# Fewer units by the seven-product scheme in the second stage, and the table sums moved to POOL, in a fused neighbourhood-attention layer

## The chip, the core and the metric

The kernel runs on one core of a Trainium2 chip. The core has a matrix engine (TensorE, PE in the profile, with its weight loads as PEld), three engines for elementwise work (VectorE or DVE, ScalarE or ACT, GpSimd or POOL), and a queue processor (SyncE, SP) from which this kernel issues nearly all of its transfers. TensorE writes only into PSUM, eight banks of 128 x 512 float32 values here, which VectorE or ScalarE must empty before a bank can be used again. Each engine works through its own instructions in program order, and engines wait for each other on semaphores. The metric is the device time of one execution in microseconds (us); less is better.

## The reference

What must be computed is one layer (DEPTH is 1, so the second mixer is not reached): an RMS norm, one projection into query, key, value and gate, an attention over an 8 x 16 neighbourhood on a grid of 32 rows by 64 columns with a learned bias per head, a gate, an output projection, the residual and a last RMS norm, all in float32.

```python
S, D, H, HD = 2048, 1024, 16, 64          # tokens, width, heads, head size

def rmsnorm(x, g):
    y = x * rsqrt(mean(x * x, -1) + 1e-6)
    return y * g

h = rmsnorm(x, norm_0)
q, k, v, gate = split(h @ w_in_0, 4)       # w_in_0: (1024, 4096)
# for every query of the grid: keys of 8 rows by 16 columns around it (clipped at the border)
s = q . k / sqrt(64) + rpb_0[head, row offset, column offset]
o = softmax(s) @ v
x = x + (o * silu(gate)) @ w_out_0
out = rmsnorm(x, norm_f)
```

## The kernel before

**Precision.** Every float32 operand of a matmul is split into a rounded high part and the rest (`h` and `l`: ScalarE copies to the high part, then a subtraction gives the low part), and a product is three matmuls: h.h, h.l and l.h.

**Units and stages.** The projection is cut into *units* `(kind, j)`: kind is k, q, g or v, and j (0 to 3) picks four heads, that is two of the eight head pairs p. The tokens are four chunks of 512, two for each stage.

- *Stage one* (`stage_one`, up to about 416 us with the values of stage two) computes the values of all heads and all twelve units k, q, g for chunks 0 and 1.
- *Stage two* (`stage_two`) does the same for chunks 2 and 3, but only for the units in `units_two` (L224): j = 0 and 1, so six units.
- The other six units of chunks 2 and 3 (`halves`, L225) are left as *filler* for the attention.

The units of both stages go through `seven_products` (L388): for two blocks of weights by two chunks it forms seven sums or differences of blocks, so that seven products of 12 matmuls (84) take the place of eight (96). The sums of weights (L410), the splits (L403, L404), and the additions on the results (L428, L432, L438, L439) are elementwise work for it. The filler does its units in the plain way, 96 matmuls for a unit (`group`, L356; lines L365, L367, L369), from weights that `use_item` splits when they are due (L177, L178).

**The attention** is a loop of 64 *pieces* (and two iterations to drain it): `order` (L878) lists row tiles (p, T) of a head pair p and a quarter T of the grid, and each has two pieces of two column blocks. T = 0 comes first for all p, then T = 1 and 2, then T = 3. In iteration i:

- `begin(i)` queues loads: on an even i the keys of the next row tile, in each the value tiles of piece i (L923).
- `feed` issues filler matmuls, 45% of the piece's amount, `middle(i)` follows, then the other 55%. `amount` (L1248) is 768 / 48 = 16 matmuls in the first 48 pieces and 354 / 18 = 19.7 in the last ones. When the units are used up (after 576 matmuls), `feed` goes on with the output projection (`outputs`, L1226 to L1230).
- `middle(i)`, on even i, splits the queries (`split_q`; `ql` at L499) and, where the head pair or the type of row tile is new, makes its *table* with `bias` (L940): six sums `em` (L948) of a bias tile `e` and a mask, for three column types and two heads, three on POOL and three on VectorE. It also queues the load of the next head pair's `e` (L936).
- then `normalise(i - 1)` (VectorE's reciprocal L982, POOL's L984), `turns(i - 2)` (transposes on TensorE, L989, copied from PSUM by ScalarE, L1013, and VectorE, L1014, into `pta`), `scores(i)` (TensorE L966 into four banks `s`; VectorE L973 adds the table `em`; ScalarE's exp L976), and `values(i - 2)` (TensorE L1034).

**Evictions and late work.** A filler product that is done is emptied by VectorE (`tmp`, L326 or L328), and one of the output by L1138 (`y`). Work that should come later is put in a list with a due mark that counts matmuls (`store`): for an output row block the root of the norm on VectorE (L1154 to L1161) is due at 12, the scale by it (L1168 on VectorE, L1169 on ScalarE, L1170 on POOL) at 16, the store at 44. POOL also makes the low part of some weights (L178), of w_out (L183) and, in the attention, of keys (L352).

**Buffers.** Each pool has a fixed number of buffers: `vp` 6 (value tiles, and landing places in the stages), `ep` 2 (tables' `e`, and one result of the seven products).

Of the kernel before, what the change touches and what calls it, by code (L numbers as in the profile page):

```python
# [10 lines left out]
F32 = mybir.dt.float32  # L11
# [59 lines left out]
def build(ctx, tc, x, xr, xt, wg, rpb, w_out, n0, nf, masks, out):  # L71
# [19 lines left out]
    qp = pool("qp", 4)  # L91
    vp = pool("vp", 6)
    sp = pool("sp", 2)
# [3 lines left out]
    mp = pool("mp", 6)  # L97
    ep = pool("ep", 2)
    lp = pool("lp", 1)
# [58 lines left out]
    def use_item(it):  # L158
        kind, a, b = it
        state["event"] = clock[0]  # L160
        t = raws.pop(it)
        if kind == "x":
            split_x(a, b, t, (hh[a, b], hl[a, b]))
        elif kind == "w":
            u, ph = a
            if KINDS["v"] <= u < KINDS["g"]:
                t = t.rearrange("p (k c) -> p k c", c=256)
                a = u // 2 * 2, ph
                if u % 2 == 0:
# [7 lines left out]
            nc.scalar.activation(h, t, AF.Copy)  # L177
            (nc.gpsimd if (b + u) % 2 and attending[0] else nc.vector).tensor_tensor(l, t, h.bitcast(F32), OP.subtract)  # L178
        else:
            h, l = xs([128, 512], F32R, "woh"), xs([128, 512], F32R, "wol")  # L180
            woh[a, b], wol[a, b] = h, l
            nc.scalar.activation(h, t, AF.Copy)
            (nc.gpsimd if b else nc.vector).tensor_tensor(l, t, h.bitcast(F32), OP.subtract)  # L183

# [38 lines left out]

    units_two = [(k, j) for j in range(2) for k in "kqg"]  # L224
    halves = [(k, j, 1, c) for j in range(2, 4) for g in (("k", "q", "g") if j == 2 else ("k", "qg")) for c in (2, 3) for k in g]  # L225
    attending = [False]
# [107 lines left out]
    def give(kind, hp, c, tmp):  # L334
# [16 lines left out]
        nc.scalar.activation(hi, tmp, AF.Copy)  # L351
        (nc.gpsimd if attending[0] else nc.vector).tensor_tensor(lo, tmp, hi.bitcast(F32), OP.subtract)  # L352
        store(("k", hp, c), 12, lambda: (nc.sync.dma_start(k_hi[hp][:, s], hi.bitcast(F32)),
# [188 lines left out]
    def stage_one():  # L542
# [6 lines left out]
        land["x21"] = [spot[:, k] for k in range(3)] + [lp([128, 512], F32, "land")]  # L549
        slots = [(mp, 512)] * 6 + [(vp, 512)] * 2 + [(sp, 512)] * 2 + [(pa, 768)] * 2 + [(vp, 512)] * 4  # L550
        slots += [(qp, 512)] * 4 + [(kp, 960)] * 4
# [22 lines left out]
        def also(n, i):  # L574
# [15 lines left out]
            if n == 0:  # L590
# [6 lines left out]
                elif i == 1:  # L597
                    L2["x21"] = [p([128, 512], F32, "land") for p in (mp, mp, vp, vp)]
                    for k in range(4):
# [72 lines left out]
        load_rows(*halves_of(1)[4:])  # L672
        for a, b in ((0, 2), (1, 2)):
            load_v0(1, a, b)
        for b in range(4):
# [8 lines left out]
            else:  # L684
                split_v(1, 0, b)
                split_v(1, 1, b)
            if b == 1:
                for a in range(2):
                    load_v0(1, a, 3)
        for k in range(4):  # L690
# [50 lines left out]
    def stage_two():  # L741
        x12, x11, x21 = L2["x12"], L2["x11"], L2["x21"]
        x22 = [qp([128, 512], F32, "land") for _ in range(4)]
        for k in range(4):
            load_x(2, "x22", k, x22[k])
        slots = {"T2": [(mp, 512)] * 4 + [(kp, 960)] * 4,
                 "T3": [(sp, 512)] * 2 + [(pa, 768)] * 2 + [(qp, 512)] * 3 + [(lp, 512)],
                 "T4": [(vp, 512)] * 4 + [(mp, 512)] * 2 + [(vp, 512), (qp, 512)]}

# [190 lines left out]
    def bias(p, ty, cty):  # L940
# [4 lines left out]
        for s in range(2):  # L945
            t = mp([128, 512], F32, "em")[:, :n]
            EM[p, ty, cty, s] = t
            (nc.vector if s else nc.gpsimd).tensor_tensor(  # L948
                sh(t), E[p, s][:, u0 + 4:u1 + 4, v0 + 8:v1 + 8], sh(MK[0][:, m0:m0 + n]), OP.add)
# [196 lines left out]
    def finish(n):  # L1146
# [30 lines left out]
        store(("y", n), 12, root)  # L1177
        store(("y", n), 16, scale)
        store(("y", n), 44, send)
# [99 lines left out]
    def begin(i):  # L1279
        all_loads()  # L1280
        m = i // 2
        if i % 2 == 0 and m + 1 < len(order):
            kh, _, kl = LOADS[m + 1] = load_qk(*order[m + 1])
            later_loads([kh, kl], 0, 2)
        if i < N:
            p, T, cs = pairs[i]
            later_loads(load_v(p, T, cs[0]) + load_v(p, T, cs[1]), 1, 1.5)
        if i % 2 == 0 and 2 <= i <= N:
            p, T = order[m - 1]
            later_loads([lambda: load_sg(p, T)], 7, 0)  # L1290

    def middle(i):
        if i % 2 or i >= N:
            return
        m = i // 2
        p, T = order[m]
        ty = ROW_TYPE[T]
        for key in [key for key in EM if key[:2] != (p, ty)]:
            del EM[key]
        if type(QT[p, T]) is not tuple:  # L1300
            split_q(p, T)
        for cty in range(3):
# [67 lines left out]
```

## Time and profile before

| what | us |
|---|---|
| median of 3 runs (1141.05 to 1146.37) | 1145.77 |
| the profiled execution, its own time | 1150.48 |
| its span, first to last instruction | 1148.7 |
| busy PE / PEld | 1100.1 / 894.9 |
| busy DVE / ACT / POOL | 768.5 / 537.4 / 358.0 |
| first scores of the attention begin at | 533.9 |
| last scores (first of the last group) begin at | 1075.6 |

Busy time is the union of an engine's instructions. A matmul is recorded for longer than the distance to the next one, since they are pipelined, so a busy TensorE isn't one at its peak. The profile also gives the granted clock of TensorE (1 is full speed) for each stretch. In a row of the timeline, the first numbers are start and length in us, and a bracket at the end tells how long the engine was idle before it and what ended that. In a row of groups, `x576 | 186.3, 389 | 0.0` is a count, the busy time in us, the mean of one in ns, and the idle time before.

### The profile page before, as it was taken

What the parts mean: (1) busy time and instruction counts of PE and PEld (TensorE: products, weight loads), DVE (VectorE), ACT (ScalarE), POOL (GpSimd) and SP (SyncE); (2) the same over time, 40 slices, a digit from 0 to 9 for tenths busy, and PEclk for the clock granted to TensorE, in tenths of its full rate; (3) what the DMA queues carried; (4) which work ended last, traced back from release to release, by engine and by line L of the source; (5) the groups of instructions that cost most, each with busy time, mean ns of one, the idle gap of its engine ahead of it and who ended that gap; (6) DMA issues with size and microseconds to landing.
All of it is one profiled execution on the core that took longest, in us unless ns stands there. A gap on an engine that the chain in (4) does not pass through costs nothing.

```text
span 1148.7 us, 22549 instructions
## 1 busy us (share of the span) xinstructions
PE 1100.1 (96%) x7621; PEld 894.9 (78%) x7621; DVE 768.5 (67%) x1743; ACT 537.4 (47%) x1348; POOL 358.0 (31%) x439
## 2 busy tenths in 40 slices
PE   9999999999999999999899999999888899999997
PEld 6788888888888888887777777778666778877885
DVE  5376787888785357877565666657867676776644
ACT  7544433343353433334544556546655456545422
POOL 0000222222210003133653535534464444444300
PEclk9999999999999999999898989999989899998999
DMA  8634545353572335349887778789897687887542
GB/s 305 190 92 125 186 127 184 120 176 114 176 238 79 100 86 162 99 138 290 238 238 221 221 232 227 230 240 263 227 267 227 175 241 241 245 250 223 155 147 73
DMA packets 142962, 217.28 MB, mean 189 GB/s; under 512 B 18048, under 2 KB 65408, under 8 KB 142848
## 3 DMA queue, kind: packets, MB, share of 16 engines
q1 hardware_dynamic: 142704, 215.58, 62.6%
q8 instruction: 61, 1.00, 0.4%
q14 instruction: 53, 0.43, 0.1%
q10 hardware_dynamic: 144, 0.26, 0.1%
HBM read 157.05 MB, written 58.72 MB: 188 GB/s over the span
## 4 chain that ended last, share of the span: by engine, by line
PE 79%; DMA 6%; DVE 6%; ACT 4%; issue 3%; SPq 1%; POOL 0%; DVEq 0%; ACTq 0%
PE pp L421 29%; PE pv L534 11%; PE o L1034 7%; PE s L966 6%; PE po L1230 5%; PE po L1228 4%; PE po L1226 4%; PE pp L369 3%; PE ph L989 3%; PE pp L365 3%; PE pp L367 3%; DVE em L948 2%; DMA vt<-vd 1%; DMA raw<-in_wg_dram 1%; ACT x L976 1%
## 5 line engine op out<-in xcount | busy, mean ns | idle before, releaser
L439 POOL TENSOR_TENSOR tmp<-tmp,rb 128x512 f32<-128x512 f32 x54 | 88.2, 1634 | 442.9 <-DVE tmp L438 288.0
L984 POOL TENSOR_SCALAR x<-x,st 128x360 f32<-128x360 f32 (+5 forms) x256 | 143.7, 580 | 169.8 <-DVE st L982 127.2
L421 PE MATMUL pp<-h,f 128*128 128x512 f32 x576 | 186.3, 389 | 0.0
L976 ACT ACTIVATE x<-x,st 128x360 f32<-128x360 f32 (+5 forms) x256 | 151.7, 594 | 58.4 <-DVE st L973 58.4
L421 PE MATMUL pp<-t,f 128*128 128x512 f32 x648 | 155.8, 389 | 0.1
L421 PEld LDWEIGHTS pp<-t,f 128*128 128x128 f32 x648 | 121.6, 188 | 25.7 <-DVE u L432 0.6
L973 DVE CUSTOM_DVE_ANT_0 x<-s,em 128x360 f32<-128x360 f32 (+5 forms) x256 | 123.9, 537 | 5.5 <-PE s L966 2.9
L421 PEld LDWEIGHTS pp<-h,f 128*128 128x128 f32 x576 | 108.1, 188 | 22.3
L966 PE MATMUL s<-kt,qh 64*128 64x480 f32 (+5 forms) x512 | 88.5, 380 | 29.9 <-DVE y L1138 11.6
L1034 PEld LDWEIGHTS o<-pta,vt 96*64 96x64 f32 (+2 forms) x1792 | 95.9, 152 | 21.4 <-issue 11.6
L421 PE MATMUL pp<-l,f 128*128 128x512 f32 x288 | 112.0, 389 | 0.0
L1034 PE MATMUL o<-pta,vt 96*64 96x128 f32 (+4 forms) x1792 | 105.0, 275 | 3.5 <-DMA raw<-in_w_out_dram 1.0
L1230 PE MATMUL po<-wol,gh 128*128 128x512 f32 x252 | 102.5, 407 | 0.0
L1228 PE MATMUL po<-woh,gl 128*128 128x512 f32 x252 | 101.0, 401 | 0.0
L1226 PE MATMUL po<-woh,gh 128*128 128x512 f32 x252 | 101.0, 401 | 0.0
L1013 ACT ACTIVATE pta<-ph 96x256 f32<-96x256 f32 (+1 forms) x224 | 58.3, 332 | 86.2 <-PE ph L989 86.0
L1014 DVE COPY pta<-ph 128x384 f32<-128x384 f32 (+3 forms) x128 | 60.3, 511 | 53.9 <-PE ph L989 53.9
L534 PE MATMUL pv<-wh,h 128*128 128x512 f32 x256 | 88.3, 390 | 0.9 <-ACT wh L516 0.9
L534 PE MATMUL pv<-wl,h 128*128 128x512 f32 x256 | 88.0, 390 | 0.3 <-DVE wl L517 0.3
L534 PE MATMUL pv<-wh,l 128*128 128x512 f32 x256 | 88.0, 389 | 0.0
L404 DVE TENSOR_TENSOR f<-raw,f 128x512 fp32r<-128x512 f32 x90 | 72.6, 806 | 22.7 <-ACT f L403 22.7
L966 PEld LDWEIGHTS s<-kt,qh 64*128 64x128 f32 x512 | 51.4, 192 | 40.3 <-ACT pta L1013 14.5
(139 smaller groups left out, 2017.2 us busy)
## 6 DMA issues: line engine op xcount, KB each, us to landing
raw<-in_wg_dram SPq DMA_DIRECT2D x126, 256.0 KB
e<-in_rpb_dram SPq DMA_DIRECT2D x54, 240.0 KB
vt<-vd SPq DMA_DIRECT2D x256, 48.0 KB
row<-in_xr_dram SPq DMA_DIRECT2D x32, 256.0 KB
vd<-v SPq DMA_DIRECT2D x32, 256.0 KB
k_hi<-hi SPq DMA_DIRECT2D x32, 256.0 KB
k_lo<-lo SPq DMA_DIRECT2D x32, 256.0 KB
qd<-tmp SPq DMA_DIRECT2D x32, 256.0 KB
```

The costliest lines, as they stand in the source:

```text
L404: nc.vector.tensor_tensor(t[:, 1], src, t[:, 0].bitcast(F32), OP.subtract)
L421: nc.tensor.matmul(B[n, P], t[:, int(m == 2), c], x[k][int(m == 1)], start=P in (1, 6, 5) and k == 0 and m == 0, stop=k == 3 and m == 2, s ...
L439: nc.gpsimd.tensor_tensor(lay(tmp), lay(tmp), of(rb[c]), OP.mult)
L534: nc.tensor.matmul(ps[t], a[:, o], b, start=k == 0 and m == 0, stop=k == NK - 1 and m == 2)
L966: nc.tensor.matmul(pst[s], qq[a, qs], kk[a, :r1 - r0, c0:c1], start=(m == 0), stop=(m == 2))
L973: nc.vector.tensor_tensor_reduce(X[i, C][s], pst[s], EM[p, ROW_TYPE[T], COL_TYPE[C], s], -1.0, 1e38, OP.add, OP.min, st[:, s:s + 1])
L976: nc.scalar.activation(X[i, C][s], X[i, C][s], AF.Exp, bias=st[:, s:s + 1], scale=-1.0, accum_out=st[:, 2 + s:3 + s])
L984: nc.gpsimd.tensor_scalar(X[i, C][s], X[i, C][s], st[:, 4 + s:5 + s], 0.5, op0=OP.mult, op1=OP.mult)
L1034: nc.tensor.matmul(o[s * 64:s * 64 + 64, C * 128 + q0:C * 128 + q0 + nq], vt[C][:k, g - g0_, s * 64:s * 64 + 64], t[:k, at:at + nq], start ...
L1226: nc.tensor.matmul(p, gh, woh[q, j], start=(i == 0), stop=False)
L1228: nc.tensor.matmul(p, gl, woh[q, j], start=False, stop=False)
L1230: nc.tensor.matmul(p, gh, wol[q, j], start=False, stop=(i == NK - 1))
```

## The change

- `units_two` keeps j = 0 only: three units by seven products in stage two, nine plain ones as filler. `amount`, worked out from it, becomes 1056 / 48 = 22 in the first 48 pieces; the later ones keep 19.7.
- In the attention all six sums of a table are on POOL, and `bias` is called at the beginning of an even piece, in `begin`, not after 45% of its filler in `middle`. The load of the next `e` moves to `begin` too, with four `ep` buffers.
- The low parts of weights, of w_out and of keys are on VectorE alone.
- Value tiles are loaded for piece i - 1 in `begin(i)`, no longer for piece i, with four `vp` buffers. Some landing places and operands in the two stages move from `vp` to `ep`.
- Two value weights of stage one are loaded earlier, into `ev` buffers.
- The scale of an output row block is due at 24, not 16.

```diff
-    vp = pool("vp", 6)
+    vp = pool("vp", 4)
...
-    ep = pool("ep", 2)
+    ep = pool("ep", 4)
...
-            (nc.gpsimd if (b + u) % 2 and attending[0] else nc.vector).tensor_tensor(l, t, h.bitcast(F32), OP.subtract)
+            nc.vector.tensor_tensor(l, t, h.bitcast(F32), OP.subtract)
...
-            (nc.gpsimd if b else nc.vector).tensor_tensor(l, t, h.bitcast(F32), OP.subtract)
+            nc.vector.tensor_tensor(l, t, h.bitcast(F32), OP.subtract)
...
-    units_two = [(k, j) for j in range(2) for k in "kqg"]
-    halves = [(k, j, 1, c) for j in range(2, 4) for g in (("k", "q", "g") if j == 2 else ("k", "qg")) for c in (2, 3) for k in g]
+    units_two = [(k, j) for j in range(1) for k in "kqg"]
+    halves = [(k, j, 1, c) for j in range(1, 4) for g in (("k", "q", "g") if j < 3 else ("k", "qg")) for c in (2, 3) for k in g]
...
-        (nc.gpsimd if attending[0] else nc.vector).tensor_tensor(lo, tmp, hi.bitcast(F32), OP.subtract)
+        nc.vector.tensor_tensor(lo, tmp, hi.bitcast(F32), OP.subtract)
...
-        for a, b in ((0, 2), (1, 2)):
-            load_v0(1, a, b)
+        for a, b in ((0, 2), (1, 2), (0, 3), (1, 3)):
+            load_v0(1, a, b, ev([128, 512], F32, "raw") if b == 3 else None)
...
-            (nc.vector if s else nc.gpsimd).tensor_tensor(
+            (nc.gpsimd if attending[0] or not s else nc.vector).tensor_tensor(
                 sh(t), E[p, s][:, u0 + 4:u1 + 4, v0 + 8:v1 + 8], sh(MK[0][:, m0:m0 + n]), OP.add)
...
-        store(("y", n), 16, scale)
+        store(("y", n), 24, scale)
...
     def begin(i):
         all_loads()
         m = i // 2
-        if i % 2 == 0 and m + 1 < len(order):
-            kh, _, kl = LOADS[m + 1] = load_qk(*order[m + 1])
-            later_loads([kh, kl], 0, 2)
-        if i < N:
-            p, T, cs = pairs[i]
+        if i % 2 == 0 and i < N:
+            p, T = order[m]
+            ty = ROW_TYPE[T]
+            for key in [key for key in EM if key[:2] != (p, ty)]:
+                del EM[key]
+            for cty in range(3):
+                if (p, ty, cty, 0) not in EM:
+                    bias(p, ty, cty)
+            if m + 1 < len(order):
+                nx = order[m + 1]
+                LOADS[m + 1] = kh, _, kl = load_qk(*nx)
+                later_loads([kh, kl], 0, 2)
+                if nx[0] != p:
+                    later_loads(load_e(nx[0]), 4, 2)
+        if 0 < i <= N:
+            p, T, cs = pairs[i - 1]
             later_loads(load_v(p, T, cs[0]) + load_v(p, T, cs[1]), 1, 1.5)
...
     def middle(i):
...
-        p, T = order[m]
-        ty = ROW_TYPE[T]
-        for key in [key for key in EM if key[:2] != (p, ty)]:
-            del EM[key]
-        if type(QT[p, T]) is not tuple:
-            split_q(p, T)
-        for cty in range(3):
-            if (p, ty, cty, 0) not in EM:
-                bias(p, ty, cty)
+        if type(QT[order[m]]) is not tuple:
+            split_q(*order[m])
         if m + 1 < len(order):
-            nx = order[m + 1]
-            fs = load_e(nx[0]) if nx[0] != p else []
-            later_loads(fs + [LOADS[m + 1][1]], 1, 2)
+            later_loads([LOADS[m + 1][1]], 1, 0)
```

What this does to the engines' rows is shown at three places. A row is the line, the operation, and what it writes and reads, with its shape; the changed kernel's lines from `stage_one`'s end on are smaller by three, so its `em` is L945, its scale L1166.

VectorE in piece 16, the first with T = 1, from the gating of the former row tile (`og`) to the copies of `pta`; first before:

```order
L1048 TENSOR_TENSOR og<-o,sgt 128x512
L499 SCALAR_TENSOR_TENSOR ql<-qr,qh 128x512
L948 TENSOR_TENSOR em<-e,mk 128x360
L948 TENSOR_TENSOR em<-e,mk 128x480
L948 TENSOR_TENSOR em<-e,mk 128x360
L328 TENSOR_TENSOR tmp<-pp,rb 128x512
L341 SCALAR_TENSOR_TENSOR sg<-sg,tmp 128x512
L178 TENSOR_TENSOR w<-raw,w 128x512
L982 RECIPROCAL st<-st 128x2 x2
```

and in the changed kernel:

```order
L1045 TENSOR_TENSOR og<-o,sgt 128x512
L178 TENSOR_TENSOR w<-raw,w 128x512
L326 TENSOR_TENSOR tmp<-pp,rb 128x512
L352 TENSOR_TENSOR lo<-tmp,hi 128x512
L178 TENSOR_TENSOR w<-raw,w 128x512
L499 SCALAR_TENSOR_TENSOR ql<-qr,qh 128x512
L979 RECIPROCAL st<-st 128x2 x2
```

The three table sums ahead of the eviction `tmp` are gone; a second weight sum and the low part of a key have come, around the eviction.

POOL around the same table; before, with the normalisations of piece 14 ahead and those of piece 15 behind:

```order
L984 TENSOR_SCALAR x_6495<-x_6495,st 128x352
L984 TENSOR_SCALAR x_6496<-x_6496,st 128x352
L178 TENSOR_TENSOR w<-raw,w 128x512
L948 TENSOR_TENSOR em<-e,mk 128x360
L948 TENSOR_TENSOR em<-e,mk 128x480
L948 TENSOR_TENSOR em<-e,mk 128x360
L984 TENSOR_SCALAR x_6602<-x_6602,st 128x352
```

and in the changed kernel:

```order
L981 TENSOR_SCALAR x_6165<-x_6165,st 128x352
L981 TENSOR_SCALAR x_6166<-x_6166,st 128x352
L945 TENSOR_TENSOR em<-e,mk 128x360 x2
L945 TENSOR_TENSOR em<-e,mk 128x480 x2
L945 TENSOR_TENSOR em<-e,mk 128x360 x2
L981 TENSOR_SCALAR x_6280<-x_6280,st 128x352
```

Six sums stand where three stood, and the weight sum ahead of them, which waits for ScalarE, is gone.

ScalarE where the first output row block is scaled (`y`), from the query split to the copies of `pta`; before:

```order
L498 ACTIVATE qh<-qr 128x512
L1169 ACTIVATE y<-y,st_9428 128x512
L1013 ACTIVATE pta<-ph_10269 96x4x64
L1013 ACTIVATE pta<-ph_10269 72x2x64
L1013 ACTIVATE pta<-ph_10287 128x4x64
```

and in the changed kernel, where on VectorE's side the root stands ahead of the query split and no longer behind three table sums:

```order
L498 ACTIVATE qh<-qr 128x512
L1166 ACTIVATE y<-y,st_9712 128x512
L1103 ACTIVATE gh<-ograw 128x512 x2
L1138 ACTIVATE xr,st_9982<-y 128x512
L1010 ACTIVATE pta<-ph_10488 96x4x64
```

The scale still stands ahead of the copies, now with two splits of the next output operand and a square in between.

More of the change, by code (lines that the diff above doesn't have):

```diff
@@ L549, in stage_one @@
         land["x21"] = [spot[:, k] for k in range(3)] + [lp([128, 512], F32, "land")]
-        slots = [(mp, 512)] * 6 + [(vp, 512)] * 2 + [(sp, 512)] * 2 + [(pa, 768)] * 2 + [(vp, 512)] * 4
+        slots = [(mp, 512)] * 6 + [(ep, 512)] * 2 + [(sp, 512)] * 2 + [(pa, 768)] * 2 + [(vp, 512)] * 4
         slots += [(qp, 512)] * 4 + [(kp, 960)] * 4
@@ L597, in also @@
                 elif i == 1:
-                    L2["x21"] = [p([128, 512], F32, "land") for p in (mp, mp, vp, vp)]
+                    L2["x21"] = [p([128, 512], F32, "land") for p in (mp, mp, ep, ep)]
                     for k in range(4):
@@ L686, in stage_one @@
                 split_v(1, 1, b)
-            if b == 1:
-                for a in range(2):
-                    load_v0(1, a, 3)
         for k in range(4):
@@ L747, in stage_two @@
                  "T3": [(sp, 512)] * 2 + [(pa, 768)] * 2 + [(qp, 512)] * 3 + [(lp, 512)],
-                 "T4": [(vp, 512)] * 4 + [(mp, 512)] * 2 + [(vp, 512), (qp, 512)]}
+                 "T4": [(vp, 512)] * 4 + [(mp, 512)] * 2 + [(ep, 512), (qp, 512)]}
         def also(n, i):
```

## The prediction

> **What bounds the kernel now.** I read the slices of the page first, then busy time by stage, then who TensorE waits for, then the instructions just ahead of its longest waits.
>
> ```profile
> span 1148.7 us, 22549 instructions
> PE   9999999999999999999899999999888899999997
> 416.00:530.00 114.00, 114.00 (x505) 94.43 (x504) 84.47 (x114) 37.18 (x65) 28.66 (x19) 1.00 0.48 154
> 534.00:817.00 283.00, 267.35 (x2657) 214.90 (x2659) 179.59 (x540) 154.83 (x479) 131.93 (x194) 0.95 0.81 234
> 817.00:907.00 90.00, 77.97 (x775) 62.20 (x772) 63.68 (x160) 47.70 (x140) 48.30 (x59) 0.91 0.81 231
> 907.00:1076.00 169.00, 159.33 (x1501) 129.50 (x1499) 121.91 (x383) 90.58 (x269) 77.82 (x117) 0.95 0.76 228
> ```
>
> The last four rows are stages: length, then busy time of PE, weight load, DVE, ACT and POOL with instruction counts, then granted clock, DMA share and GB/s. Up to 530 us TensorE never pauses at the full clock: these stages are its own work. In the attention (534 to 1076) it idles 283 - 267.35 = 15.7, then 12.0, then 9.7 us, 37.4 in all, and its clock is below 1: 283 x 0.05 + 90 x 0.09 + 169 x 0.05 = 30.7 us of full speed lost. So **68.1 us** of the attention are stalls and what they cost in clock (0.82 us of clock for 1 us idle). Who ends the waits there, with total, times and longest:
>
> ```profile
> PE s L966 <- DVE y L1138: 11.6, 4, 4.3
> PE s L966 <- ACT pta L1013: 11.5, 8, 3.5
> PE s L966 <- DVE tmp L328: 5.6, 3, 2.7
> PE ph L989 <- POOL x L984: 3.1, 4, 1.1
> PE s L966 <- DVE ql L499: 1.1, 2, 0.6
> ```
>
> The scores wait for a PSUM bank which VectorE (y, tmp) or ScalarE (pta) has yet to empty. Why these are late, at the longest wait (first fence, DVE then PE) and at the longest of the ACT kind (DVE, ACT, PE):
>
> ```profile
> 828.02 4.17 DVE L948 TENSOR_TENSOR em<-e,mk 128x360 f32<-128x360 f32 x3
> 832.11 0.68 DVE L1138 TENSOR_TENSOR y<-po,xr 128x512 f32<-128x512 f32 x1
> ...
> 832.85 1.24 PE L966 MATMUL s<-kt,qh 64*128 64x480 f32 x4 [4.26 <-DVE y L1138]
> ```
> ```profile
> 883.44 1.54 DVE L948 TENSOR_TENSOR em<-e,mk 128x360 f32<-128x360 f32 x3
> 884.89 0.20 DVE L1154 TENSOR_SCALAR st<-st 128x1 f32<-128x1 f32 x1
> ...
> 886.94 0.72 ACT L1169 ACTIVATE y<-y,st 128x512 f32<-128x512 f32 x1 [4.14 <-DVE st L1161]
> 887.56 0.96 ACT L1013 ACTIVATE pta<-ph 96x256 f32<-96x256 f32 x4
> ...
> 888.14 1.16 PE L966 MATMUL s<-kt,qh 64*128 64x480 f32 x3 [3.49 <-ACT pta L1013]
> ```
>
> VectorE's three table sums (em, L948) stand in front of an eviction in the first; in the second they stand in front of the root, which ScalarE's scale (L1169) waits for at the head of its own queue, with the copies of pta behind it. All four waits on y and all three on tmp have three table sums right ahead of the eviction (the next two rows are one of each). So 11.6 + 5.6 us are these sums; of the 11.5, three waits have a scale in front that waited for the root, the one above and the last two rows:
>
> ```profile
> 906.37 3.77 DVE L948 TENSOR_TENSOR em<-e,mk 128x360 f32<-128x360 f32 x3
> 657.87 3.78 DVE L948 TENSOR_TENSOR em<-e,mk 128x360 f32<-128x360 f32 x3
> ...
> 946.39 0.62 PE L966 MATMUL s<-kt,qh 64*128 64x384 f32 x3 [2.42 <-ACT pta L1013]
> 1047.63 0.79 PE L966 MATMUL s<-kt,qh 64*128 64x384 f32 x3 [1.55 <-ACT pta L1013]
> ```
>
> 3.49 + 2.42 + 1.55 = 7.5 us. The 3.1 us on POOL x are normalisations queued behind POOL's weight and key sums early in the attention.
>
> **The change, part by part.**
>
> ```profile
> 415.87 114.24 PE pp L421 x504
> 737.25 0.85 PE ph L989 x23
> 744.65 0.84 PE ph L989 x22
> ```
>
> These rows are of the chain that ended last: start, length, what. *Products.* 504 matmuls in 114.24 us are 0.2267 us each. Three units by seven products go: 3 x 84 x 0.2267 = **-57.1 us**, all in a stage where TensorE is the bound. As plain products they are 3 x 96 x 0.2267 = **+65.3 us** of filler: +8.2 for 36 more matmuls. What VectorE, ScalarE and POOL save in stage two hides under TensorE there, worth nothing. Filler per piece rises from 16 to 22 matmuls in the first 48 pieces and stays at 19.7 in the last. An undisturbed piece takes 744.65 - 737.25 = 7.40 us, of which 16 x 0.2267 = 3.63 are filler; with 22 it takes 8.76, so each piece gives the other engines 1.4 us more.
>
> *Table sums to POOL, at the piece's beginning.*
>
> ```profile
> L948 POOL TENSOR_TENSOR em<-e,mk 128x360 f32<-128x360 f32 (+5 forms) x81 | 72.3, 913 | 14.1 <-DMA e<-in_rpb_dram 9.3 <-DVE st L973 4.5
> L948 DVE TENSOR_TENSOR em<-e,mk 128x360 f32<-128x360 f32 (+5 forms) x81 | 50.8, 679 | 0.0
> L984 POOL TENSOR_SCALAR x<-x,st 128x360 f32<-128x360 f32 (+5 forms) x256 | 143.7, 580 | 169.8 <-DVE st L982 127.2 <-PE ph L989 24.1 <-ACT pta L1013 11.5
> L178 POOL TENSOR_TENSOR w<-raw,w 128x512 fp32r<-128x512 f32 x10 | 12.8, 1282 | 24.6 <-ACT w L177 24.6
> L178 DVE TENSOR_TENSOR w<-raw,w 128x512 fp32r<-128x512 f32 x14 | 11.2, 803 | 11.5 <-ACT w L177 11.5
> L352 DVE TENSOR_TENSOR lo<-tmp,hi 128x512 fp32r<-128x512 f32 x24 | 16.3, 681 | 2.7 <-ACT hi L351 2.7
> L183 DVE TENSOR_TENSOR wol<-raw,woh 128x512 fp32r<-128x512 f32 x8 | 5.5, 689 | 5.5 <-ACT woh L182 5.5
> ```
>
> The 162 sums are 27 tables of six. VectorE keeps two of its 81, so it loses about 50 us. POOL gets six in a row: 6 x 0.913 = 5.5 us, and with four normalisations of 0.58 (2.3 us) behind them 7.8 us against a piece of 8.76; the next piece has only 2.3 us for POOL. The first four sums (3.7 us) must be there when the scores end the piece, the normalisations a piece later. So POOL hides them if it starts on them within 8.76 - 3.7 = 5 us; they cost nothing then, and the rival below prices the other case.
>
> *Other sums to VectorE.* It gets 22 more weight sums (14 to 36), 8 of keys and 8 of w_out: 22 x 0.803 + 8 x 0.681 + 8 x 0.689 = 28.6 us, but single ones between evictions, where 4.17 us stood in a lump. Net it loses some 21 us in the attention.
>
> *Root and scale.* The scale is put into the queue 24 instead of 16 matmuls after the last row, so 12 x 0.2267 = 2.7 us behind the root instead of 0.9. The root needs 886.94 - 884.89 = 2.05 us (rows above), so the scale no longer waits for it: ScalarE's 7.5 us go. The store behind it comes at 44 matmuls as before.
>
> *Loads.* Value tiles are asked for one piece later (two pieces, some 17 us, ahead), with four buffers.
>
> ```profile
>   PEld o L1034: 0.4, 2
> 557.98 6.58 DMA vt<-vd
> ```
>
> TensorE waited 0.4 us for them in all; the longest stretch of the chain on one is 6.58 us, well within 17. SP issues the loads of a new piece where it did, in the same order with the tables' loads earlier, so what queues behind a late buffer is the same: I take 0, bounded by 0.4 us less and 6.58 more (one such wait). The two value weights loaded earlier, and buffers that vp hands to ep, are in stage one, whose products waited 0.9 us for a weight split (row below): 0, at most 1 either way.
>
> ```profile
> L534 PE MATMUL pv<-wh,h 128*128 128x512 f32 x256 | 88.3, 390 | 0.9 <-ACT wh L516 0.9
> ```
>
> *The sum.* Causes removed: 11.6 + 5.6 + 7.5 + 3.1 = 27.8 us of waits. That is 74% of 37.4, with its clock 27.8 x 1.82 = 50.6 us. Left are 17.5 us; the longer pieces may cover more, VectorE's new sums may cost some, and I let these cancel. What remains is unknown between 0 (all cover) and 68.1 (as many waits anew). Sum: -57.1 + 65.3 - 50.6 = **-42.4 us**. The profiled execution took 1150.48 us with a span of 1148.7; the median of the runs is 1145.8, so 4.7 lower. 1145.8 - 42.4 = **1103**; by bounds 1145.8 + 8.2 - 68.1 = 1086 and 1145.8 + 8.2 = 1154.
>
> **The rivals.**
>
> *VectorE is as late by its new sums (half the gain).* For it: pieces of the changed order have w, tmp, lo, w, ql in one go, 0.8 + 0.7 + 0.7 + 0.8 + 0.85 = 3.8 us, near the 4.17 lump, and VectorE slows beside POOL: the lump's sums took 1.39 each against 0.679 in the mean. Against it: evictions stand between, not behind. Half of the 50.6: 1145.8 + 8.2 - 25.3 = 1129. The Trainium skill (SBUF — State Buffer, "Who interferes with whom") says that a VectorE instruction with two SBUF inputs and a GpSimd instruction that reads SBUF exclude each other for a whole instruction; by that, POOL's six sums in a row hold up VectorE's splits, which speaks against this change. The 1.39 beside 0.679 agrees.
>
> *Only the products count.* If every stall finds a successor, the 36 matmuls remain: 1154. For it: TensorE reads 9 in nearly all slices, so more work for it looks like more time. Against it: those slices hide 37 us idle. The Trainium skill (Perfetto Trace Analysis, "Identifying the Most-Contended Engine") would have the most occupied engine relieved first, which speaks against adding matmuls; it also says that matmul busy time misleads, and the weight-load column agrees, 94.43 of 114 before the attention and 62.20 of 90 within.
>
> *POOL is late with the tables (slower).* If a table's load is late (9.3 us of such waits, above), or if each sum takes (8.76 - 2.3) / 4 = 1.6 us or more behind the former normalisations, the scores wait in all 27 pieces with a new table. With 1.5 us each: 27 x 1.5 x 1.82 = 73.7 us of new stalls in place of 50.6 removed: 1145.8 + 8.2 - 50.6 + 73.7 = 1177. It decides from a start 5 us into the piece. Against it: tables are asked for two pieces ahead, and POOL loses its 26 other sums (w alone 1.28 each).
>
> **How the numbers follow.** Forecast 0.64 (1088 to 1117), half the gain 0.22, products alone 0.07, POOL late 0.07. The likeliest gives 1103. The range runs from the lower bound, 1086, to just above the half gain, 1134, and leaves out the last two cases and tails. A measurement tells some 0.5% (5.7 us) from no change. Faster by more than that: 0.64 + 0.22 = 0.86. Of the products alone, half falls within 0.5%: same 0.04, slower 0.10.
>
> **What would show it.** Right: the first scores some 57 us earlier (near 477); table sums on POOL alone but two; waits on y and tmp gone or below 3 us; granted clock 0.97 or more in the attention; pieces of 8.8 us. Wrong: waits of scores behind w or wol on DVE (half gain), table sums releasing L970 (POOL late), or waits for vt.

## The result, and the profile after

The changed kernel takes **1103.12 us** (median of 4 runs, 1100.11 to 1105.24) where the kernel before takes 1146.07 (4 runs, 1141.05 to 1149.36): the ratio is 0.9627, with a 95% interval of 0.9585 to 0.9669. The forecast was 1103.0. Its profiled execution took 1102.79 us. The page of it begins so (busy time with its share of the span and the count of instructions, then slices in tenths):

```profile
span 1101.0 us, 22543 instructions
PE 1080.7 (98%) x7657; PEld 883.6 (80%) x7657; DVE 732.7 (67%) x1663; ACT 531.5 (48%) x1336; POOL 378.5 (34%) x483
PE   9999999999999999999999999999999999999997
```

36 matmuls more than before are busy for 19.4 us less (1100.1 before). The 8s that stood in TensorE's slices in the attention are gone. By stage, with the columns of the same view of before (length; busy time of PE, weight load, DVE, ACT and POOL; clock; DMA share; GB/s):

```profile
479.00:784.00 305.00, 301.62 (x2874) 245.24 (x2872) 190.97 (x544) 161.27 (x491) 138.63 (x211) 0.99 0.79 234
784.00:869.00 85.00, 81.17 (x801) 66.17 (x797) 63.33 (x153) 50.41 (x144) 52.09 (x65) 0.96 0.85 257
869.00:1028.00 159.00, 155.83 (x1528) 127.83 (x1525) 117.15 (x364) 91.56 (x271) 99.63 (x141) 0.99 0.79 241
```

The three are the attention. TensorE idles 3.4 + 3.8 + 3.2 = 10.4 us there, against 37.4 before, and the clock, at 0.99, 0.96 and 0.99 (0.97 or more was forecast), loses 305 x 0.01 + 85 x 0.04 + 159 x 0.01 = 8.0 us, against 30.7. Stalls and clock together are 18.4 us; they were 68.1. In these figures and those below, a clock is printed to 0.01, so over some 540 us the clock's part is uncertain by 2.7 us.

The first and the last weight load for scores (min, median and longest in ns, then first and last start in us), and who TensorE waits for in the attention (total, times, longest):

```profile
L963 PEld LDWEIGHTS s<-kt,qh x512: 182/186/330, 478.8 to 1028.7; 64*128 64x128 f32 x171
```
```profile
PE o L1031 <- DVE pta L1011: 4.6, 5, 2.0
PE o L1031 <- DMA vt<-vd: 1.9, 2, 1.6
PE s L963 <- DVE tmp L326: 1.5, 1, 1.5
PE s L963 <- ACT pta L1010: 1.2, 1, 1.2
```

The waits on y (11.6 us) and on POOL's x (3.1) no longer appear, tmp went from 6.2 (5.6 on L328, 0.6 on L326) to 1.5, and pta on ScalarE from 11.5 to 1.2. What leads now is the values (L1031), which wait for VectorE's copies of pta.

The tables run on POOL as the change says. The group of table sums (count, then busy us and mean ns of one, then POOL's idle time before them), and POOL at one table (start, length, what):

```profile
L945 POOL TENSOR_TENSOR em<-e,mk 128x480 f32<-128x480 f32 (+5 forms) x160 | 140.8, 915 | 5.0 <-DVE st L970 5.0
```
```profile
602.33 2.03 POOL L981 TENSOR_SCALAR x<-x,st 128x264 f32<-128x264 f32 x4 [6.06 <-DVE st L979]
604.31 5.51 POOL L945 TENSOR_TENSOR em<-e,mk 128x360 f32<-128x360 f32 x6
613.84 2.02 POOL L981 TENSOR_SCALAR x<-x,st 128x352 f32<-128x352 f32 x4 [4.02 <-DVE st L979]
```

Six sums take 5.51 us, and POOL then idles 4.02 us before it is wanted again. But that the sums are well hidden here does not show that moving them won the time. The runs below ask that.

### The profile page after: what moved, and what is told of

Same layout as the page of the kernel before. It is cut to its first block, busy times and chain, and to the rows that moved or that the text cites. A ratio compares the mean times of both kernels' runs of the same rounds, so it can differ in the third digit from the quotient of the medians.

```text
span 1101.0 us, 22543 instructions
## 1 busy us (share of the span) xinstructions
PE 1080.7 (98%) x7657; PEld 883.6 (80%) x7657; DVE 732.7 (67%) x1663; ACT 531.5 (48%) x1336; POOL 378.5 (34%) x483
## 2 busy tenths in 40 slices
DMA packets 142962, 217.29 MB, mean 197 GB/s; under 512 B 18048, under 2 KB 65408, under 8 KB 142848
## 4 chain that ended last, share of the span: by engine, by line
PE 88%; DVE 5%; DMA 3%; issue 2%; ACT 1%; POOL 1%; SPq 0%; DVEq 0%; POOLq 0%
PE pp L421 24%; PE pv L534 16%; PE o L1031 7%; PE s L963 6%; PE pp L369 6%; PE pp L367 6%; PE pp L365 5%; PE po L1227 5%; PE po L1223 4%; PE po L1225 4%; PE ph L986 4%; ACT x L973 1%; PE zp L1242 1%; DVE gl L1104 1%; DMA sgt<-sgd 0%
## 5 line engine op out<-in xcount | busy, mean ns | idle before, releaser
L439 POOL TENSOR_TENSOR tmp<-tmp,rb 128x512 f32<-128x512 f32 x45 | 73.5, 1634 | 399.2 <-DVE tmp L438 358.4
L421 PE MATMUL pp<-h,f 128*128 128x512 f32 x480 | 155.4, 389 | 0.0
L945 POOL TENSOR_TENSOR em<-e,mk 128x480 f32<-128x480 f32 (+5 forms) x160 | 140.8, 915 | 5.0 <-DVE st L970 5.0
L421 PE MATMUL pp<-t,f 128*128 128x512 f32 x540 | 129.8, 389 | 0.1
L970 DVE CUSTOM_DVE_ANT_0 x<-s,em 128x360 f32<-128x360 f32 (+5 forms) x256 | 123.8, 538 | 5.1 <-PE s L963 2.0
L421 PEld LDWEIGHTS pp<-t,f 128*128 128x128 f32 x540 | 101.3, 188 | 21.5 <-DVE u L432 0.6
L369 PE MATMUL pp<-h,w 128*128 128x512 f32 x288 | 115.9, 403 | 0.0
L367 PE MATMUL pp<-l,w 128*128 128x512 f32 x288 | 114.2, 397 | 0.0
L365 PE MATMUL pp<-h,w 128*128 128x512 f32 x288 | 113.6, 394 | 0.0
L1031 PEld LDWEIGHTS o<-pta,vt 96*64 96x64 f32 (+2 forms) x1792 | 86.0, 139 | 24.2 <-DVE pta L1011 10.2
L421 PEld LDWEIGHTS pp<-h,f 128*128 128x128 f32 x480 | 90.1, 188 | 18.8
L1031 PE MATMUL o<-pta,vt 96*64 96x128 f32 (+4 forms) x1792 | 95.2, 258 | 7.5 <-DVE pta L1011 4.6
L421 PE MATMUL pp<-l,f 128*128 128x512 f32 x240 | 93.4, 389 | 0.0
```

The costliest lines, as they stand in the source:

```text
L365: nc.tensor.matmul(p, wh[w, b][:, cols], hh[k, c], start=(k == 0), stop=False)
L367: nc.tensor.matmul(p, wh[w, b][:, cols], hl[k, c], start=False, stop=False)
L369: nc.tensor.matmul(p, wl[w, b][:, cols], hh[k, c], start=False, stop=(k == NK - 1))
L421: nc.tensor.matmul(B[n, P], t[:, int(m == 2), c], x[k][int(m == 1)], start=P in (1, 6, 5) and k == 0 and m == 0, stop=k == 3 and m == 2, s ...
L945: (nc.gpsimd if attending[0] or not s else nc.vector).tensor_tensor(sh(t), E[p, s][:, u0 + 4:u1 + 4, v0 + 8:v1 + 8], sh(MK[0][:, m0:m0 + n ...
L1031: nc.tensor.matmul(o[s * 64:s * 64 + 64, C * 128 + q0:C * 128 + q0 + nq], vt[C][:k, g - g0_, s * 64:s * 64 + 64], t[:k, at:at + nq], start ...
```

## The experiments

A stall figure below is idle time of TensorE from the first to the last scores, plus the length times what the clock lacks to 1, from the one row of the stage view that is shown. A row that begins up to 5.4 us after the first scores leaves out a stretch without a pause and at the full clock. Taken from one row too, the 68.1 of before would read 69.9 and the 18.4 after 21.4; that is the rounding. The medians of the kernel before were 1145.37 us beside the first four runs, 1142.88 beside e5 to e8, and 1146.18 beside e9 to e12.

### The parts of the change, each alone

**e1: the units alone.** The kernel before, with only three units by seven products:

```diff
-    units_two = [(k, j) for j in range(2) for k in "kqg"]
+    units_two = [(k, j) for j in range(1) for k in "kqg"]
```

(`halves` goes with it as in the change; all sums, loads and due marks are as before.)

> The kernel before with only units_two and halves of the change (three units by seven products, nine as filler). Theory A (the stalls come from table sums on VectorE and the scale behind the root): these stay, the 36 more matmuls cost 8.2 us, the longer pieces cover at most a third of the 68 us of stalls; 1131 to 1154 us, and waits of the scores on y, tmp and pta of 20 us or more. Rival B (the longer pieces are what hides the stalls): 1110 us or less, these waits below 10 us.

Measured: 1132.22 us, ratio 0.9890 (0.9860 to 0.9921). The attention's row, and the waits that lead in it:

```profile
479.00:1056.00 577.00, 551.17 (x5204) 447.61 (x5203) 387.94 (x1102) 303.56 (x905) 272.46 (x376) 0.97 0.79 230
```
```profile
PE s L966 <- ACT pta L1013: 6.9, 8, 2.4
PE o L1034 <- DVE pta L1014: 5.1, 3, 2.9
...
PE s L966 <- DVE y L1138: 3.5, 2, 2.1
```

So 36 matmuls more, for which the sum had +8.2 us, make the kernel 13.2 us *faster*. Stalls fell from 68.1 to 25.8 + 577 x 0.03 = 43.1 us, with no sum moved. Waits on y are 3.5 us, not 11.6: a lump of sums that stood in the way in a piece with 16 filler matmuls is mostly covered in one with 22. The rest stays: 3.5 us on y and 6.9 on pta are waits that the change as a whole removes or brings to 1.2. In the last 16 pieces, whose filler is 19.7 matmuls in both kernels, even the lengths stay. The waits of 2.42 and 1.55 us on pta that the prediction shows at 946.39 and 1047.63 are in e1 too:

```profile
926.14 0.76 PE L966 MATMUL s<-kt,qh 64*128 64x384 f32 x3 [2.42 <-ACT pta L1013]
1028.68 0.88 PE L966 MATMUL s<-kt,qh 64*128 64x384 f32 x3 [1.55 <-ACT pta L1013]
```

So it is the longer piece that covers. The result fits neither expectation whole: the time is at the fast end of theory A's range, but the waits on y, tmp and pta are 6.9 + 3.5 + 0.9 = 11.3 us and not 20.

**e2: everything but the units.** The changed kernel, with six units by seven products and 16 filler matmuls in a piece (the lines of e1 the other way round):

```diff
-    units_two = [(k, j) for j in range(1) for k in "kqg"]
+    units_two = [(k, j) for j in range(2) for k in "kqg"]
```

> The changed kernel with six units by seven products again (pieces of 16 filler matmuls). Theory A: 36 matmuls fewer, 8.2 us saved, and POOL's 7.8 us of a new table are spread over two pieces of 7.4 us, so 1095 us, or 1100 with some new waits. Rival B (the longer pieces are what hides the stalls): the stalls come back, 1115 us or more.

Measured: 1126.12 us, ratio 0.9834 (0.9806 to 0.9862).

```profile
537.00:1050.00 513.00, 482.08 (x4897) 390.31 (x4895) 344.29 (x1022) 291.00 (x883) 289.91 (x418) 0.97 0.83 241
```
```profile
PE o L1031 <- DMA vt<-vd: 16.2, 12, 3.3
```

The moved sums do what was said of them (y and tmp are below 2 us, and not among the leading waits), but in these shorter pieces the value tiles come late: 16.2 us in 12 waits, where before had 0.4 and the changed kernel has 1.9. Stalls are 30.9 + 513 x 0.03 = 46.3 us. Of the 50.6 us that I had put down to the causes removed, the median shows 19.3.

**e5: the table sums alone.** The kernel before, with all table sums of the attention on POOL, still in the middle of the piece:

```diff
-            (nc.vector if s else nc.gpsimd).tensor_tensor(
+            (nc.gpsimd if attending[0] or not s else nc.vector).tensor_tensor(
```

> The kernel before with all six table sums of the attention on POOL and nothing else (one line). Theory A (three table sums in one lump on VectorE, in front of evictions and of the root, make most of the stalls): the waits on y and tmp go, 11.6 + 5.6 us, half of the 7.5 us behind the scale and the clock with them, about 38 us: 1100 to 1115 us. Rival B (without longer pieces other waits take their place): 1125 us or more.

Measured: 1135.21 us (6 runs), ratio 0.9922 (0.9886 to 0.9958). The attention's row, the leading waits, and POOL ahead of the longest:

```profile
534.00:1060.00 526.00, 496.14 (x4942) 398.78 (x4940) 336.52 (x1006) 295.03 (x889) 326.81 (x447) 0.96 0.81 239
```
```profile
PE ph L989 <- POOL x L984: 9.1, 12, 3.9
PE s L966 <- ACT pta L1013: 7.9, 6, 2.5
PE s L966 <- ACT qh L498: 5.1, 4, 2.9
PE s L966 <- DVE ql L499: 4.3, 6, 1.6
```
```profile
818.30 6.38 POOL L948 TENSOR_TENSOR em<-e,mk 128x360 f32<-128x360 f32 x6
824.64 3.70 POOL L183 TENSOR_TENSOR wol<-raw,woh 128x512 fp32r<-128x512 f32 x3
828.33 4.76 POOL L984 TENSOR_SCALAR x<-x,st 128x480 f32<-128x480 f32 x8
```

The waits on y and tmp are gone, as the cause in the prediction said they would be. Two others stand in their place. POOL's own queue is one: six sums, then three sums of w_out, then the normalisations that the transposes wait for, 3.9 us in the case shown. That is the forecast's rival of a late POOL, in a kernel whose POOL still has its other sums. The second hardly stood in the way before (ql 1.1 us): the scores wait for the halves of the queries (qh and ql, 9.4 us together).

### Engine, place and due marks within the change

Five runs each take a part of the change back, the units staying at three.

**e3, e4 and e8.** e3 gives VectorE back half of the table sums, at the piece's beginning. e4 leaves all of them on POOL but calls `bias` after 45% of the filler again. e8 puts the scale back to 16.

```diff
# e3
-            (nc.gpsimd if attending[0] or not s else nc.vector).tensor_tensor(
+            (nc.vector if s else nc.gpsimd).tensor_tensor(
# e4: this block from begin() to the end of split_q in middle()
-            for cty in range(3):
-                if (p, ty, cty, 0) not in EM:
-                    bias(p, ty, cty)
# e8
-        store(("y", n), 24, scale)
+        store(("y", n), 16, scale)
```

> The changed kernel with every second table sum on VectorE again, still at the piece's beginning. Theory A (sums on VectorE in front of evictions): some of the stalls return, but at the beginning fewer evictions stand behind them; 1108 to 1125 us, and waits of the scores on tmp or y reappear. Rival C (the place at the beginning is what helps, not the engine): within 4 us of 1103.

> The changed kernel with all table sums on POOL, but issued after 45% of the piece's filler as before. Theory A: POOL's queue order hardly changes and POOL waits for no matmul, so within 4 us of 1103. Rival C (the place is what helps): 1110 us or more.

> The changed kernel with the scale due at 16 again. Theory A' (the scale waits for the root also without the table sums in front, 16 - 12 = 4 matmuls or 0.9 us for a root of 2.05 us): waits of the scores on pta come back in the last 20 pieces, 1106 to 1115 us. Rival (the sums in front of the root were the whole delay): within 3 us of 1103.

Measured: e3 1101.65 us, 0.9622 (0.9597 to 0.9647); e4 1103.00, 0.9635 (0.9604 to 0.9666); e8 1101.41, 0.9613 (0.9581 to 0.9645). All three intervals contain the change's 0.9627. With 22 matmuls in a piece, a lump on VectorE at the beginning or one on POOL in the middle is covered: moving either the engine or the place is enough. No run puts back both and nothing else. The nearest is e1, with VectorE's lump in the middle and the old splits, scale and loads besides, and it is some 30 us slower (0.9890). In e8 one wait behind the scale is back, 1.55 us at 902.15, and it costs nothing that these runs can tell.

**e7 and e12.** e7 is the change with the old loads and buffers (and the sums on POOL in the middle, as the old `middle` has them): the kernel before with the lines of e1 and e5, the three splits on VectorE and the scale at 24. e12 is the change with the splits shared with POOL as before.

```diff
# e12, the same for woh and for the keys' lo
-            nc.vector.tensor_tensor(l, t, h.bitcast(F32), OP.subtract)
+            (nc.gpsimd if (b + u) % 2 and attending[0] else nc.vector).tensor_tensor(l, t, h.bitcast(F32), OP.subtract)
```

> The change (three units by seven products, nine as filler; sums, splits, scale) with the loads and buffers of before. Theory D: pieces of 22 matmuls cover the later loads but for the 1.9 us that waited for value tiles, so 1098 to 1103 us. Were the loads or the buffers themselves a gain of the change, it would be 1108 us or more.

> The changed kernel with the low parts of weights, w_out and keys shared with POOL again as before. If POOL with six table sums (5.5 us) and normalisations (2.3 us) in a piece of 8.8 us has no room for sums of 1.3 us: waits on POOL x or on the tables, 1108 to 1118 us. If it has: within 4 us of 1103.

Measured: e7 1103.98 us, 0.9634 (0.9607 to 0.9662); e12 1106.21, 0.9647 (0.9587 to 0.9706). The old order of loads does as well as the new, and the splits bring nothing that these runs can tell (the medians, 1106.21 and 1103.12, were taken at different times, and the intervals overlap).

### What holds the shorter pieces

**e6: e7 with six units.** The kernel before, with all elementwise edits (table sums on POOL, the three splits on VectorE, scale at 24) and nothing else. Against e7 only the units differ, and the two ran on one chip.

> Six units by seven products and the loads and buffers of before (value tiles asked three pieces ahead, six buffers), with all sums and splits on the engines of the change and the scale at 24. Theory D (with pieces of 16 matmuls the later loads of the value tiles take what is gained, 16.2 us of waits and their clock in the run with six units, whose median was 1126): 1095 to 1102 us, and waits for value tiles below 3 us. Rival B (short pieces bring stalls of other kinds): 1115 us or more.

Measured: 1130.20 us, 0.9874 (0.9834 to 0.9914).

```profile
538.00:1052.00 514.00, 488.46 (x4874) 392.03 (x4872) 348.28 (x1025) 291.35 (x883) 293.69 (x415) 0.96 0.83 242
```
```profile
PE s L966 <- DVE ql L499: 8.2, 10, 1.9
PE s L966 <- ACT qh L498: 3.9, 4, 1.1
```

Stalls are 25.5 + 514 x 0.04 = 46.1 us, and at their head stand the query halves. Why they are late shows in the view of the tile qr, which ScalarE (qh) and VectorE (ql) read. It lists how long the engine that reads or writes it sat idle, and until what. ScalarE's row in e6, in the kernel before, and in e7 and e1, the two with 22 matmuls in a piece (e1 has no row of a DMA, only VectorE's):

```profile
  DMA qr<-qd: 18.4, 11
```
```profile
  DMA qr<-qd: 8.5, 6
```
```profile
  DMA qr<-qd: 3.2, 2
```
```profile
  ACT qh L498: 30.3, 26
```

ScalarE stood 18.4 us, in 11 pieces, before a query tile that had not landed; with the same loads in the same order but 1.4 us more filler in a piece it stood 3.2 us in two, and in e1 never. The kernel before has 8.5 us of it already, though its scores waited only 1.1 us on ql. The table tiles are late in the same way; POOL's row in the view of the tile e, in e6:

```profile
  DMA e<-in_rpb_dram: 39.4, 25
```

Before it is 9.3 us in three, in e7 9.6 in nine, and none in e1. A piece that gets shorter as its waits go brings the loads' lateness to light. Something else may add to the waits on ql: it takes 1.05 us in the mean in e6, beside POOL's six sums, and 0.85 before. But in e11 below, with the same sums on POOL, it takes 0.96, and that kernel is fast.

**e9: is it the query load alone?** e6 with the query load first in the even piece:

```diff
-            kh, _, kl = LOADS[m + 1] = load_qk(*order[m + 1])
+            kh, q, kl = LOADS[m + 1] = load_qk(*order[m + 1])
+            q()
...
-            later_loads(fs + [LOADS[m + 1][1]], 1, 2)
+            later_loads(fs, 1, 2)
```

> The kernel of e6 (six units, old loads, 1130 us) with the query load of the next row tile put first in the piece, ahead of its keys, instead of behind the tables after 45% of the filler. Theory E (in pieces of 16 matmuls the loads are as long as the piece, and the one that comes last, the queries, holds up the scores: 12.1 us of waits on ql and qh): these waits go, with their clock some 20 us, 1106 to 1115 us. Rival E' (the whole list of loads is too long for the piece, so another load is late instead): 1120 to 1130 us.

Measured: 1139.39 us (10 runs), 0.9942 (0.9908 to 0.9976): above both ranges, and no better than e6.

```profile
538.00:1058.00 520.00, 489.79 (x4878) 395.01 (x4878) 350.14 (x1025) 291.51 (x883) 297.58 (x415) 0.95 0.83 239
```
```profile
PE s L966 <- DVE ql L499: 7.2, 5, 3.5
PE o L1034 <- issue: 6.4, 4, 3.6
```

ScalarE no longer waits for a query tile at all, yet stalls are 30.2 + 520 x 0.05 = 56.2 us. Now other loads are later. POOL's row in the view of the tile e and VectorE's in that of the gate tile sgt, and then VectorE and TensorE at the longest wait on ql:

```profile
  DMA e<-in_rpb_dram: 64.7, 28
```
```profile
  DMA sgt<-sgd: 18.0, 6
```
```profile
739.24 0.69 DVE L1048 TENSOR_TENSOR og<-o,sgt 128x512 f32<-128x512 f32 x1 [6.96 <-DMA sgt<-sgd]
739.85 0.68 DVE L499 SCALAR_TENSOR_TENSOR ql<-qr,qh 128x512 fp32r<-128x512 f32 x1
...
740.58 0.67 PE L966 MATMUL s<-kt,ql 64*128 64x360 f32 x2 [3.52 <-DVE ql L499]
```

VectorE stood 6.96 us before the gating (og) for a gate tile that had not landed, with ql behind it in its queue. In e6 the gate tiles cost it 6.2 us in four. At the values (L1034) "issue" names no releaser, so what was late there the trace does not say. The theory that the query load alone holds the pieces fell; what is left of it is that the list of loads as a whole is too long for a piece with 16 filler matmuls.

**e11: fewer loads.** e6, with no load of `e` after the second head pair's:

```diff
         def rows(s):
+            if (1, s) in E:
+                E[p, s] = E[1, s]
+                return
             t = (pool_ or ep)([128, 512], F32, "e")[:, :480]
```

> The kernel of e6 without the loads of the bias tiles e after the second head pair's (50 transfers of 240 KB left out; all later tables are made from that pair's tile). Theory E or E' (loads fill the short pieces): 1095 to 1112 us, waits on qh and ql below 4 us. Rival F (in short pieces the engines' own work is too long, loads or not): 1122 us or more.

Measured: 1101.15 us, 0.9606 (0.9548 to 0.9663). TensorE's and the other engines' instructions are as many as in e6; 12.3 MB fewer are moved (204.98 against 217.29). The attention's row, and the leading waits:

```profile
538.00:1030.00 492.00, 477.58 (x4934) 384.90 (x4931) 346.88 (x1033) 293.41 (x893) 291.42 (x419) 0.99 0.80 228
```
```profile
PE s L969 <- ACT pta L1016: 2.6, 6, 0.9
PE o L1037 <- issue: 2.2, 2, 1.2
PE s L969 <- DVE ql L499: 2.2, 3, 0.9
```

Stalls fall from 46.1 to 14.4 + 492 x 0.01 = 19.3 us, as low as in the change, and the ratio by 0.027, some 30 us, with six units and 16 matmuls in a piece. So what holds e6 is its loads. This run does not tell *how* they hold it: it takes away bytes, the time that SP needs to issue 50 transfers, POOL's 39.4 us before table tiles, and the times that SP stands before an `e` load whose buffer is still being read. The view of SP's waits in e6 has this last one:

```profile
SPq L936 <- POOL em L948: 3.3, 2, 2.0
```

(Another 5.3 us at this line are put down to POOL's x, which does not read e.) e7 has 9.6 us of this wait and is fast, which speaks against it. The DMA share hardly moved (0.83 to 0.80), which speaks against bandwidth alone; no run parts what is left.

**e10: a length in between.** The change with a fourth unit, the keys of j = 1, by seven products (`halves` goes with it), so that the amount is (96 x 8 + 192) / 48 = 20 matmuls in a piece:

```diff
-    units_two = [(k, j) for j in range(1) for k in "kqg"]
+    units_two = [("k", 0), ("q", 0), ("g", 0), ("k", 1)]
```

> The changed kernel with a fourth unit by seven products (keys of j = 1), eight as filler, so 20 matmuls for a piece. Products alone: 2.7 us less, 1100 us. Theory E (the piece's length covers the loads; 16 matmuls cost 31 us of stalls more than 22): between, 1103 to 1112 us.

Measured: 1105.37 us, 0.9635 (0.9574 to 0.9696).

```profile
PE o L1031 <- DMA vt<-vd: 6.3, 4, 2.6
```

It does 12 matmuls less than the change, 2.7 us of work at 0.2267 each, and shows no gain, though its interval could hide one of that size. Waits for value tiles are 6.3 us at 20 matmuls in a piece and 16.2 at 16 (e2). At 22, with the same loads, they are 1.9 in the change but run from 0.4 (e8) to 4.9 (e3), so only the 16.2 stands out.

## Why the prediction was right, and where it was not

- **What bounds the kernel** held: 68.1 us of stalls were the store that the change draws on, and 49.7 of them went (forecast 50.6).
- **The products** held. The first scores come at 478.8 us, 55.1 earlier than at 533.9 (forecast 57.1). From the first to the last weight load for scores it is now 549.9 us, and 533.9 to 1076.4 is 542.5 before: 7.4 more, where +65.3 of filler less 50.6 gave 14.7. That is 7.3 us shorter than forecast, although 0.9 us less of stalls went than the sum had. The rounding of the clock, 2.7 us in each kernel, may hold 5.4 of these 8.2 us; the rest I cannot place. Against its own profiled execution the sum was 5.3 us short (1150.48 - 1102.79 = 47.7), while the medians differ by 43.0. That the number comes out to 0.1 us is luck; that it lies in the likeliest range is not. The transposes of neighbouring pieces begin 8.2 to 9.3 us apart in most of the first 48, where I had 8.8.
- **The table sums on POOL** are hidden as worked out: 915 ns each for a forecast of 913, two left on VectorE, and VectorE's additions to the scores (L970) waited 0.2 us for them in all. Of the kernels with all six sums on POOL, it comes late only where short pieces and its 26 other sums come together: TensorE waits 9.1 us for its normalisations in e5, but 0.5 in e6, which has the short pieces alone, and 0.7 in e12, which has the other sums alone.
- **VectorE's new sums** cost what was forecast one by one, and hold next to nothing. The groups of w, lo and wol after (count, busy us, mean ns):

```profile
L178 DVE TENSOR_TENSOR w<-raw,w 128x512 fp32r<-128x512 f32 x36 | 28.8, 802 | 15.6 <-ACT w L177 15.6
L352 DVE TENSOR_TENSOR lo<-tmp,hi 128x512 fp32r<-128x512 f32 x32 | 21.9, 685 | 10.6 <-ACT hi L351 10.6
L183 DVE TENSOR_TENSOR wol<-raw,woh 128x512 fp32r<-128x512 f32 x16 | 11.6, 743 | 6.7 <-ACT woh L182 6.7
```

  The counts are those of the forecast, 36, 32 and 16. That VectorE has net 21 us less to do in the attention was wrong, though: its three stages sum to 371.5 us (190.97 + 63.33 + 117.15), and before to 365.2. I counted the sums and not what three more plain units bring VectorE there: 12 more evictions alone are 8.2 us (36 for 24). It did no visible harm; they come singly.
- **The rival "half the gain"** rested on such splits being held up beside POOL. They are: while POOL ran the six sums of 604.31 to 609.82, one split took 1.81 us and the next ones of its line 0.68:

```profile
608.55 1.81 DVE L178 TENSOR_TENSOR w<-raw,w 128x512 fp32r<-128x512 f32 x1 [0.93 <-ACT w L177]
610.29 0.68 DVE L326 TENSOR_TENSOR tmp<-pp,rb 128x512 f32<-128x512 f32 x1
...
612.28 0.68 DVE L178 TENSOR_TENSOR w<-raw,w 128x512 fp32r<-128x512 f32 x1
```

  The Trainium skill's rule (SBUF — State Buffer, "Who interferes with whom") agrees with this pair of rows. The eviction behind it (L326) came some 1.6 us late, as the last of its 24 matmuls ended near 608.7. TensorE paid little for it: 0.29 us before the scores at 613.62, for ql. The mean of L178 did not rise; that of ql did, from 0.854 us to 0.949, and it is 0.689 in e3, where POOL has half the sums. In the change all this costs next to nothing.
- **The scale at 24** was credited with 7.5 us of waits. They are gone, but e8 has 16, gets only the 1.55 of them back, and is no slower. The longer piece alone does not remove them: e1 keeps the 2.42 and the 1.55. What stood in the way was mostly the sums in front of the root, as the prediction has it, and the due mark adds little.
- **The loads** were put at nothing. In the change that holds (1.9 us of waits for vt, e7 the same time with the old loads). At the old length of the pieces it does not: 16.2 us in e2.
- **The step that failed** is the one in the sum that credits 27.8 us of waits, 50.6 with their clock, to the causes removed, and then says that "the longer pieces may cover more, VectorE's new sums may cost some, and I let these cancel". By the runs, the removal alone is worth 12.7 us (e6) to 19.3 (e2), and the longer pieces alone 13.2 + 8.2 = 21.4 (e1), where I had 0. The medians of e6 and e1 add up to 25.9 us; both edits together (e7) make 38.9. The half-widths of the three intervals, 3.1 to 4.6 us, make 6.6 together, so these 13 us are more than scatter. Two things each hold the scores: elementwise work that stands in a lump, and loads that need longer than a piece with 16 filler matmuls. Taking the first away shortens the pieces and brings out the second, as e6 shows; giving the pieces 22 matmuls covers the second and a part of the first. With the loads covered, the removal is worth 38.9 - 13.2 = 25.7 us (e7 against e1), twice what it is worth at 16 matmuls. I took the loads at TensorE's 0.4 us of before, and did not ask what they would be once the pieces got shorter; ScalarE's 8.5 us before query tiles were the sign of it. I had the right total because what the sums could not deliver, the filler did.
- **The rival "only the products count"** (1154) fell by e1: the products alone give 1132. The Trainium skill's advice to optimize the most occupied engine first (Perfetto Trace Analysis, "Identifying the Most-Contended Engine") points the wrong way here if it is read as taking work off that engine, since TensorE was 96% busy and got more to do. The next section of that page of the Trainium skill, "Optimization Strategy", says that interleaving regimes with different bounds may help; e1 agrees, moving work from a stage without a pause into one with 37.4 us of them.

No run beats the change by more than can be told: e3 and e8 are 1.5 to 1.7 us lower, taken at other times. The two together were not tried. e11 is no rival, as it makes less than the whole layer.

## What to carry to other kernels

Where a matrix engine alternates between a stage that it bounds and one in which it waits, work that is cheaper in the first can still be better placed in the second: here 36 matmuls more cost 8.2 us of work and cover 25 us of stalls. Before a wait is credited to the instruction that ends it, ask what would be late next if the piece were shorter by that wait, and look through the transfers of one piece above all; a load that waits for nothing today may only be covered by today's other stalls. And an edit is best judged both with and without its companions: each of two causes looked small alone, and the engine on which the sums run, which looked decisive, did not matter once the pieces were longer and the sums stood at a piece's beginning (e3).

## What was unexpected of the hardware

In the prediction I gave each idle microsecond of TensorE the 0.82 us of lost clock that the attention of before shows. That is no constant. In e6 it is 20.6 us of clock beside 25.5 us idle (0.81) and in e9 26.0 beside 30.2 (0.86), but in e2 only 15.4 beside 30.9 (0.50), with some 0.1 of rounding in each. e2 idles more than e6 and loses less clock; its longest group of waits is at the values, where those of e6 and e9 are at the scores or at both. The place alone is not it: e11 waits mostly at the scores, in pauses of at most 1.3 us, and loses 4.9 us beside 14.4 idle (0.34, with 0.17 of rounding). Whether the length or the spacing of the pauses makes the difference, no run here was made to tell.
